# Value and gate projections of the HGRN2 layer moved ahead of its heads, with seven block products for eight

## The chip, the cores and the metric

The kernel runs on one core of a Trainium2 chip. A core has five engines that run side by side, each through its own instructions in program order: TensorE (PE; its weight loads are shown apart as PEld), VectorE (DVE), ScalarE (ACT), GpSimdE (POOL) and SyncE (SP). They wait for each other through semaphores. SP and POOL also issue the DMA transfers here. The metric is the device time of one execution in microseconds. Three runs of the kernel before gave 3575.16, 3577.86 and 3580.52 us; the median is 3577.86 us.

## The reference

A backbone of two layers over 1024 latent tokens and 256 context tokens, model width 1024. Layer 0 has neighbourhood attention and mLSTM heads and isn't touched. Layer 1, cut to what matters (`h` is the normalized, modulated input; T = 1024 latent, 256 context tokens):

```python
q, f_fwd, f_bwd, i, z = split(h @ w_in_c, (2048,) * 5)       # 16 heads of 128 columns each
f = lb + (1 - lb) * sigmoid(f_pre)                            # per direction; k = 1 - f, decay f
q = silu(q)
# per head and direction: S_t = f_t * S_(t-1) + k_t (x) i_t ;  o_t = q_t . S_t
# the state starts from the context tokens; both directions are summed
o = rms(o_fwd + o_bwd, h_norm_c)                              # per head
y = (o * silu(z)) @ w_out_c ;  x = x + gate * y
```

`i` is the value path (V below), `z` the gate path. Only latent tokens leave layer 1, so of the context tokens F and V are needed, not Q and Z.

## The kernel before, in words

Float32 products are made of three passes: every operand is split into a high part and a low remainder of a rounded type, and high x high, high x low and low x high are summed in PSUM. `split` (line 61) makes the two parts: a cast on ACT, a subtraction on DVE. `wblock` and `wring` load and split weights; `wring` uses a ring of four slabs (`wl`, `wh`) of 128x512. `dense` (lines 120 to 122) issues the three matmuls of each of the eight 128-row steps.

`hh` and `hl` hold the transposed `h` of layer 1, all 1280 tokens, in SBUF. In `build`, layer 1 is a loop over 16 heads:

- `hg_proj(h)`: F of both directions and Q, transposed (128 columns of the head by tokens). Eight tiles in PSUM tag `mm`, which has two banks. F goes to `gF` (two halves of 512 tokens) and, for the context, to `gFc`, which has one buffer. ACT takes the sigmoid, DVE scales it. The weights of head 0's F are loaded early, in the last part of layer 0, where its first products are placed too.
- `hg_intra(h)`: inside blocks of 128 tokens, the triangular product A of Q and K by seven levels of doubling blocks (`hg_level`), for two halves of 512 tokens (upper half first). At each level ACT copies a selection of K to `gksel`, TensorE makes four products from it and Q (line 900), DVE writes the masked result into A (line 910, `copy_predicated`) and multiplies K and Q by decays (line 918). Level 0 writes A by a plain multiplication (line 906) and is followed by the diagonal (`hg_diag`). At the end K is transposed (line 879).
- `hg_vz(h)`: V of the context, and for eight tiles of 128 latent tokens V and Z together (256 columns, 24 matmuls a tile); ACT copies V and takes the sigmoid of Z, DVE multiplies (line 821).
- `hg_ctx(h)`: the state of the context, with two scans on DVE that read `gFc` (lines 833, 834).
- `hg_scan(h)`: the states over eight blocks in both directions, the sum in PSUM tag `acc`, the norm (squares on ACT, the root on POOL), times the gate into `gyn` (line 973), four transposes each half (line 976), and a store.

The order on each engine is not that of the code: the scheduler places instructions by priority (earlier code first) and by its own model of time, so products of `hg_vz(h)` stand between the levels of `hg_intra(h)`, and `hg_proj(h+1)` between the steps of `hg_scan(h)`. The order is fixed when the program is built.

Of the kernel before, what the change touches and what calls it, by code (L numbers as in the profile page):

```python
# [9 lines left out]
F32 = mybir.dt.float32  # L10
F32R = mybir.dt.float32r
# [32 lines left out]
class Prog:  # L44
# [727 lines left out]
    def hg_proj(self, h, pool, w=None):  # L772
# [7 lines left out]
        if w:  # L780

            todo.sort(key=lambda x: x[1] == 0)
        w = w or [None, None]
# [17 lines left out]

    def hg_vz(self, h, st, pool):
        nc, a = self.nc, self.a
        col = lambda i: a["wc"][:, i * 2048 + h * P : i * 2048 + (h + 1) * P]
        w = self.wblock(pool, "wz", [col(3), col(4)], KD, 256)
        v = self.t(pool, [P, NT, P], F32, "gv", 2)
        z = self.t(pool, [P, NT - 2, P], F32, "gz", 1)
        ps = self.ps("mm", [P, CTX])
        self.proj_tr(ps, w, 0, LAT, CTX)
        vT = self.t(pool, [P, CTX], F32, "gEc", 1)  # L810
        nc.scalar.copy(vT, ps)
        pt = self.ps("tr", [P, 2, P])
        for j in range(2):
            nc.tensor.transpose(pt[:, j, :], vT[:, j * P : (j + 1) * P], self.ident)
        nc.scalar.copy(v[:, 8:10, :], pt)
        for tt in range(8):
            ps = self.ps("mm", [P, 256])
            self.proj_nat(ps, w, tt, 0, 256)
            nc.scalar.copy(v[:, tt, :], ps[:, 0:P])
            nc.scalar.activation(z[:, tt, :], ps[:, P:256], AF.Sigmoid)  # L820
            nc.vector.tensor_tensor(out=z[:, tt, :], in0=z[:, tt, :], in1=ps[:, P:256], op=ALU.mult)
        st["v"], st["z"] = v, z
# [63 lines left out]
    def hg_level(self, H, lev, pool):  # L886
# [9 lines left out]
        qp = pick(Q)  # L896
        pa = self.ps("s", [P, 4, P])
# [34 lines left out]
    def hg_scan(self, h, st, halves, S, pool, y):  # L932
# [13 lines left out]
        for c in range(8):  # L946
# [22 lines left out]
            self.rsqrt(ss, ss, 1.0 / P)  # L969
            pt = self.ps("tr", [P, 4, P])  # L970
            for i in range(4):
                yn = self.t(pool, [P, P], F32, "gyn", 2)
                nc.vector.scalar_tensor_tensor(
                    out=yn, in0=o4[:, i, :], scalar=ss[:, i : i + 1], in1=z[:, c - 3 + i, :], op0=ALU.mult, op1=ALU.mult
                )
                nc.tensor.transpose(pt[:, i, :], yn, self.ident)
# [5 lines left out]
    def build(self):  # L982
        tc, nc, a = self.tc, self.nc, self.a
        dma = nc.sync.dma_start
        with ExitStack() as es:
# [9 lines left out]
            self.x1 = self.scratch(dr, "x1", [T, D])  # L995
            self.md_all = self.scratch(dr, "md", [20, T, 256])
# [111 lines left out]
            lk = self.fp = l1.enter_context(tc.tile_pool(name="hgk", bufs=1))  # L1108
            with tc.tile_pool(name="op0", bufs=2) as op, ExitStack() as wl:
# [37 lines left out]
                wf = [self.wring([a["wc"][:, 2048 : 2048 + P]], P), None]  # L1147
# [9 lines left out]
                wf[1] = self.wring([a["wc"][:, 4096 : 4096 + P]], P)  # L1157

            with l1:
                pool = l1.enter_context(tc.tile_pool(name="hg", bufs=2))  # L1160
                self.rawp = pool
                l1.enter_context(self.pp.phase(s=3, acc=1))
                st = self.hg_proj(0, pool, wf)
# [33 lines left out]
class _W:  # L1197
# [5 lines left out]
    def part(self, t, k):  # L1203
        return t[k // self.step][:, k % self.step * self.n : (k % self.step + 1) * self.n]
# [123 lines left out]
```

## Time and profile before

| what | value |
|---|---|
| median of three runs | 3577.86 us (3575.16 to 3580.52) |
| profiled execution: span | 3582.2 us |
| PE busy | 3517.0 us, 98% |
| DVE busy | 2216.3 us, 62% |
| ACT busy | 1419.4 us, 40% |
| POOL busy | 456.2 us, 13% |
| mean granted TensorE clock | 0.992 |
| HBM read, written | 241.49 MB, 59.30 MB |

The span is that of one profiled execution, from its first to its last instruction; its own time is that span, 4.3 us above the median of the runs. A row of a timeline gives start, length, engine, source line, operation, output and input by the program's names, and shape. Two rows of one engine can overlap, since the length holds the way through the pipeline; the distance of their starts is what one costs the engine when it has no gap. A row of stretches gives each engine's busy time with the number of instructions, then the granted clock of TensorE and the DMA share. The heads of layer 1 run from about 1955 to 3425 us; layer 1's output product follows.

### The profile page before, as it was taken

What the parts mean: (1) busy time and instruction counts of PE and PEld (TensorE: products, weight loads), DVE (VectorE), ACT (ScalarE), POOL (GpSimd) and SP (SyncE); (2) the same over time, 40 slices, a digit from 0 to 9 for tenths busy, and PEclk for the clock granted to TensorE, in tenths of its full rate; (3) what the DMA queues carried; (4) which work ended last, traced back from release to release, by engine and by line L of the source; (5) the groups of instructions that cost most, each with busy time, mean ns of one, the idle gap of its engine ahead of it and who ended that gap; (6) DMA issues with size and microseconds to landing.
All of it is one profiled execution on the core that took longest, in us unless ns stands there. A gap on an engine that the chain in (4) does not pass through costs nothing.

```text
span 3582.2 us, 65593 instructions
## 1 busy us (share of the span) xinstructions
PE 3517.0 (98%) x24954; PEld 3223.1 (90%) x24954; DVE 2216.3 (62%) x5976; ACT 1419.4 (40%) x3493; POOL 456.2 (13%) x752
## 2 busy tenths in 40 slices
PE   8999999999999999998899999999999999999998
PEld 5879999999999999997788999999999999999877
DVE  5646676666744765655556666666666666666753
ACT  5545555445533333433354333333333333333431
POOL 2222222222211212201010000000000000000000
PEclk9999999999999999999999999999999999999999
DMA  5532222232234434324742111111111111111263
GB/s 211 173 99 77 83 71 81 72 90 76 80 96 145 127 94 140 116 73 149 221 145 77 36 36 34 36 36 36 36 33 36 30 36 36 33 33 36 77 192 117
DMA packets 323051, 305.25 MB, mean 85 GB/s; under 512 B 29016, under 2 KB 280088, under 8 KB 322608
## 3 DMA queue, kind: packets, MB, share of 16 engines
q1 hardware_dynamic: 290704, 217.44, 20.7%
q0 software_dynamic: 32032, 83.61, 6.9%
q8 instruction: 197, 3.23, 0.4%
q14 instruction: 118, 0.97, 0.1%
HBM read 241.49 MB, written 59.30 MB: 84 GB/s over the span
## 4 chain that ended last, share of the span: by engine, by line
PE 85%; issue 6%; DMA 4%; DVE 2%; POOL 1%; ACT 1%; SPq 0%; POOLq 0%; DVEq 0%; ACTq 0%
PE mm L122 18%; PE mm L120 18%; PE mm L121 18%; PE s L900 6%; PE acc L677 2%; PE tr L657 2%; PE mm L731 2%; PE mm L732 2%; PE mm L733 2%; PE acc L461 2%; PE s L470 2%; DMA mld<-md 1%; PE acc L451 1%; PE s L929 1%; PE acc L953 1%
## 5 line engine op out<-in xcount | busy, mean ns | idle before, releaser
L122 PE MATMUL mm<-wh,hl 128*128 128x256 f32 x2560 | 749.6, 293 | 0.3 <-DVE hl L253 0.3
L120 PE MATMUL mm<-wh,hh 128*128 128x256 f32 x2560 | 747.0, 292 | 0.0
L121 PE MATMUL mm<-wl,hh 128*128 128x256 f32 x2560 | 745.9, 291 | 0.0
L122 PEld LDWEIGHTS mm<-wh,hl 128*128 128x128 f32 x2560 | 489.1, 191 | 11.1 <-issue 4.1
L120 PEld LDWEIGHTS mm<-wh,hh 128*128 128x128 f32 x2560 | 489.3, 191 | 7.7 <-issue 1.5
L121 PEld LDWEIGHTS mm<-wl,hh 128*128 128x128 f32 x2560 | 489.2, 191 | 7.1 <-issue 0.5
L120 PE MATMUL mm<-hh,wh 128*128 128x512 f32 (+1 forms) x1216 | 448.3, 369 | 0.0
L121 PE MATMUL mm<-hl,wh 128*128 128x512 f32 (+1 forms) x1216 | 448.3, 369 | 0.0
L122 PE MATMUL mm<-hh,wl 128*128 128x512 f32 (+1 forms) x1216 | 448.1, 368 | 0.0
L122 PE MATMUL mm<-wzh,hl 128*128 128x256 f32 x1024 | 295.3, 288 | 0.0
L120 PE MATMUL mm<-wzh,hh 128*128 128x256 f32 x1024 | 294.2, 287 | 0.0
L121 PE MATMUL mm<-wzl,hh 128*128 128x256 f32 x1024 | 293.9, 287 | 0.0
L895 ACT COPY gksel<-gK 128x512 f32<-128x512 f32 x224 | 149.3, 667 | 315.5 <-PE s L900 159.7
L122 PEld LDWEIGHTS mm<-hh,wl 128*128 128x128 f32 x1216 | 229.7, 189 | 31.4
L120 PEld LDWEIGHTS mm<-hh,wh 128*128 128x128 f32 x1216 | 229.7, 189 | 31.1
L121 PEld LDWEIGHTS mm<-hl,wh 128*128 128x128 f32 x1216 | 229.7, 189 | 30.7
L900 PE MATMUL s<-gQ,gksel 128*128 128x128 f32 x1792 | 254.9, 284 | 0.0
L900 PEld LDWEIGHTS s<-gQ,gksel 128*128 128x128 f32 x1792 | 231.4, 191 | 1.3
L71 ACT CAST wh<-wraw 128x512 fp32r<-128x512 f32 x242 | 148.6, 620 | 202.3 <-PE mm L121 122.5
L731 PE MATMUL mm<-woh,yh 128*128 128x512 f32 x524 | 209.4, 400 | 11.9 <-issue 9.7
L72 DVE TENSOR_TENSOR wl<-wraw,wh 128x512 fp32r<-128x512 f32 x242 | 165.3, 689 | 87.3 <-ACT wh L71 84.9
L733 PE MATMUL mm<-woh,yl 128*128 128x512 f32 x524 | 209.4, 400 | 0.0
(316 smaller groups left out, 7463.0 us busy)
## 6 DMA issues: line engine op xcount, KB each, us to landing
wraw<-yd SPq DMA_DIRECT2D x144, 256.0 KB
wraw<-in_wab_dram SPq DMA_DIRECT2D x112, 256.0 KB
md<-ev POOLq DMA_DIRECT2D x100, 256.0 KB, 2.7
wraw<-in_wc_dram SPq DMA_DIRECT2D x96, 256.0 KB
adar<-in_wada_dram POOLq DMA_DIRECT2D x32, 512.0 KB, 4.6
wraw<-in_wc_dram SPq DMA_DIRECT2D x128, 128.0 KB
adar<-in_wada_dram SPq DMA_DIRECT2D x16, 512.0 KB
wraw<-in_wab_dram SPq DMA_DIRECT2D x64, 128.0 KB
```

The lines of the kernel that those rows point to most:

```text
L71: nc.scalar.copy(hi, x)
L72: nc.vector.tensor_tensor(out=lo, in0=x, in1=hi.bitcast(F32), op=ALU.subtract)
L120: mm(ps, lhsT=lh(k), rhs=rh(k), start=(k == 0), stop=False)
L121: mm(ps, lhsT=lh(k), rhs=rl(k), start=False, stop=False)
L122: mm(ps, lhsT=ll(k), rhs=rh(k), start=False, stop=(k == nk - 1))
L461: nc.tensor.matmul(num, lhsT=qc[:, j, :], rhs=C[d][:, j, :], start=False, stop=(j == 1))
L470: nc.tensor.matmul(u, lhsT=st["k"][c][:, j * P : (j + 1) * P], rhs=vw, start=True, stop=True)
L657: nc.tensor.transpose(pt[:nk, i, :], pr[:, o : o + nk], self.ident)
L731: mm(ps, lhsT=yh[:, k, :], rhs=w.h(kk), start=(kk == 0), stop=False)
L733: mm(ps, lhsT=yl[:, k, :], rhs=w.h(kk), start=False, stop=(kk == 8 * len(qs) - 1))
L895: nc.scalar.copy(ksel.rearrange("p (b s i) -> p b s i", s=2, i=h), pick(K))
L900: nc.tensor.matmul(pa[:, c, :].rearrange("p (b s i) -> p b s i", s=2, i=h), lhsT=ksel[:, c * P : (c + 1) * P], rhs=qp[:, c * nbc : (c + 1) ...
```

## The change

V and Z of all heads are computed before the first head and written to a DRAM scratch `vzd`; a head reads its 128 columns of each back (`hg_vz`). Only V of the context is still computed in the head.

The product is done in eight blocks of 256 columns of V and the same 256 of Z. In block 0 (`q_plain`) it is done as before. In the others (`q_seven`) it is seen as a product of 2x2 blocks: tokens 0 to 511 and 512 to 1023 by the two halves of the inner dimension, and those halves by V and Z. Seven block products (each four token tiles, 12 matmuls of 256 columns a tile) and sums replace eight. The sums on the token side (`q_sums`: four matrices, in high and low parts) are made once, those on the weight side (`q_form`) in each block. Results go through `q_out` (sum, for Z also sigmoid and product) to `vzd`.

In the heads: the gated output overwrites the gate (`gz`, now two buffers) and is transposed by a new function `hg_y`, after the projections of the next head. At level 6 (`lev == 6`, blocks of 64 tokens) ACT copies the selection of Q to a buffer of its own, as it does with K, and the matmuls read the copy. `gF` and `gFc` lie in the heads' pool; head 0's early F weights are replaced by the V weights of block 0.

```diff
-        F = [self.t(p, [P, 2, 512], F32, "gF", 1) for p in (pool, self.fp)]
-        Fc = self.t(self.fp, [P, 2, CTX], F32, "gFc", 1)
+        F = [self.t(pool, [P, 2, 512], F32, "gF", 2) for _ in range(2)]
+        Fc = self.t(pool, [P, 2, CTX], F32, "gFc", 1)
...
+    def q_sums(self, pool):
...
+        for i in range(4):
+            q = lambda x, k, c: x[:, k : k + 4, (i + c) * P : (i + c + 1) * P]
+            o = slice(i * P, (i + 1) * P)
+            def part(n, r):
+                nc.scalar.copy(S[n][0][:, :, o], r)
+                tt(S[n][1][:, :, o], r, S[n][0][:, :, o].bitcast(F32), ALU.subtract)
...
+    def q_form(self, raw, n, add=None):
+        w = _W([], [], 2, 256)
+        for i in range(2):
+            if add:
+                self.nc.vector.tensor_tensor(out=raw[n][i], in0=raw[n][i], in1=raw[add][i], op=ALU.add)
+            w.lo.append(self.t(self.wp, [P, 512], F32R, "wl", self.slabs))
+            w.hi.append(self.t(self.wp, [P, 512], F32R, "wh", self.slabs))
+            self.split(w.hi[i], w.lo[i], raw[n][i])
+        return w
+
+    def q_mul(self, ps, a, w, first, last):
+        mm = self.nc.tensor.matmul
+        ah, al = a
+        for k in range(4):
+            mm(ps, lhsT=ah[:, k, :], rhs=w.h(k), start=first and k == 0, stop=False)
+            mm(ps, lhsT=ah[:, k, :], rhs=w.l(k), start=False, stop=False)
+            mm(ps, lhsT=al[:, k, :], rhs=w.h(k), start=False, stop=last and k == 3)
...
+    def q_seven(self, j, S, pool):
...
+        for i, ps in product(lambda i: self.q_h(i, 0), self.q_form(raw, "11")):
+            u[i] = self.t(pool, [P, 256], F32, "qu", 4)
+            nc.scalar.copy(u[i], ps)
+        for i, ps in product(lambda i: self.q_h(i, 1), self.q_form(raw, "21")):
+            self.q_out(pool, i, j, 0, u[i], ps, ALU.add)
+        for i, ps in product(s("1"), self.q_form(raw, "11", "12")):
+            m5[i] = ps
+        for i, ps in product(s("2"), self.q_form(raw, "11", "22")):
+            tt(out=u[i], in0=u[i], in1=ps, op=ALU.add)
+            v[i] = self.t(pool, [P, 256], F32, "qv", 4)
+            tt(out=v[i], in0=m5[i], in1=u[i], op=ALU.subtract)
+        for i, ps in product(s("3"), self.q_form(raw, "12", "22")):
+            self.q_out(pool, i + 4, j, 1, v[i], ps, ALU.subtract)
+            tt(out=u[i], in0=u[i], in1=ps, op=ALU.add)
+        for i, ps in product(lambda i: self.q_h(i + 4, 1), self.q_form(raw, "11", "21")):
+            self.q_out(pool, i + 4, j, 0, u[i], ps, ALU.add)
+        for i, ps in product(s("4"), self.q_form(raw, "22")):
+            self.q_out(pool, i, j, 1, v[i], ps, ALU.add)
...
     def hg_vz(self, h, st, pool):
-        w = self.wblock(pool, "wz", [col(3), col(4)], KD, 256)
...
+        for t, i in ((v, 0), (z, 1)):
+            nc.sync.dma_start(
+                out=t[:, 0:8, :], in_=self.vzd[i, :, h * P : (h + 1) * P].rearrange("(c p) f -> p c f", p=P)
+            )
...
-        for tt in range(8):
-            ps = self.ps("mm", [P, 256])
-            self.proj_nat(ps, w, tt, 0, 256)
-            nc.scalar.copy(v[:, tt, :], ps[:, 0:P])
-            nc.scalar.activation(z[:, tt, :], ps[:, P:256], AF.Sigmoid)
-            nc.vector.tensor_tensor(out=z[:, tt, :], in0=z[:, tt, :], in1=ps[:, P:256], op=ALU.mult)
...
+        if lev == 6:
+            qsel = self.t(pool, [P, n], F32, "gksel", 3).rearrange("p (b s i) -> p b s i", s=2, i=h)
+            nc.scalar.copy(qsel, qp)
+            qp = qsel
...
+    def hg_y(self, h, st, pool, y):
+        nc = self.nc
+        for c in (0, 4):
             pt = self.ps("tr", [P, 4, P])
             for i in range(4):
+                nc.tensor.transpose(pt[:, i, :], st["z"][:, c + i, :], self.ident)
...
             with l1:
+                self.nq = 0
+                with tc.tile_pool(name="qv", bufs=1) as pool, self.pp.phase(sa=4):
+                    self.q_plain(0, early, pool)
+                    S = self.q_sums(pool)
+                    for j in range(1, 8):
+                        self.q_seven(j, S, pool)
...
                 for h in range(16):
                     hv = self.hg_intra(st, pool)
                     self.hg_vz(h, st, pool)
                     S = self.hg_ctx(st, pool)
-                    self.hg_scan(h, st, hv, S, pool, self.yd2)
+                    self.hg_scan(h, st, hv, S, pool)
+                    done = st
                     if h < 15:
                         st = self.hg_proj(h + 1, pool)
+                    self.hg_y(h, done, pool, self.yd2)
```

More of the change, by code (lines that the diff above doesn't have):

```diff
@@ L1146, in build @@
                 self.slabs = 4
-                wf = [self.wring([a["wc"][:, 2048 : 2048 + P]], P), None]
+                early = []
+                for k in range(2):
+                    rows = a["wc"][k * 512 : (k + 1) * 512, 3 * 2048 : 3 * 2048 + 256]
+                    early.append(self.wblock(self.wp, "w", [rows], 4, 256, op, ring=self.slabs))
                 for tt in [8, 9, 4, 5, 6, 7, 0, 1, 2, 3]:
```

104 lines of the change are left out of this document (89 added, 15 removed).

## The prediction

> **What bounds the kernel now.** I read the page first, then stretches of layer 1, then one head in order of time.
>
> ```profile
> span 3582.2 us, 65593 instructions
> PE 3517.0 (98%) x24954; PEld 3223.1 (90%) x24954; DVE 2216.3 (62%) x5976; ACT 1419.4 (40%) x3493; POOL 456.2 (13%) x752
> PE   8999999999999999998899999999999999999998
> ```
> TensorE is busy nearly everywhere. The busy time of stretches (columns: stretch, its length, then each engine) says the same of the layer boundary (second row), of five heads (first) and of the inside of one head (last):
>
> ```profile
> 2500.00:2961.00 461.00, 461.00 (x3252) 430.37 (x3251) 301.80 (x750) 149.94 (x366) 21.38 (x30) 1.00 0.12 35
> 1900.00:1950.00 50.00, 50.00 (x259) 42.94 (x258) 30.28 (x76) 23.98 (x55) 2.20 (x5) 1.00 0.26 78
> 2139.60:2176.20 36.60, 36.60 (x319) 36.60 (x318) 30.55 (x80) 14.27 (x35) 0.60 (x1) 1.00 0.02 9
> L833 DVE TENSOR_TENSOR_SCAN gEc<-gFc,gzero x16: 683/684/684, 1990.8 to 3371.9; 128x255 f32<-128x255 f32 x16
> ```
> L833 runs once a head, so a head takes (3371.9 - 1990.8) / 15 = 92.1 us, all of it TensorE's. The stretch 2139.60 to 2176.20 is one head's `hg_intra` from the lower half's level 0 to the two context scans of `hg_ctx`. There DVE works 30.55 of 36.6 us: TensorE leads only because V and Z products fill the places where it would wait for DVE. The same stretch for the tile `wzl`, one of the three matmuls of each product step:
>
> ```profile
> 2139.60:2176.20 36.60, 16.70 (x58) 10.93 (x58) 0.00 (x0) 1.00 0.02 9
> 2079.85 0.28 PE L120 MATMUL mm<-wzh,hh 128*128 128x256 f32 x1
> 2081.98 0.28 PE L120 MATMUL mm<-wzh,hh 128*128 128x256 f32 x1
> ```
> So 3 x 58 = 174 fill matmuls stand in it. Between the two timeline rows lie 18 steps in 2.13 us: a 256-wide matmul holds TensorE for 0.118 us. The fill is 174 x 0.118 = 20.5 us of the 36.6.
>
> **The change, part by part.**
>
> *Products.* Before, V and Z take 16 heads x 8 tiles x 24 = 3072 matmuls. After, the plain block has 2 x 8 x 24 = 384 and the seven others 7 products x 4 tiles x 12 = 336 each, 2736 in all. TensorE saves 336 x 0.118 = **39.6 us**. The context rows of V (24 matmuls a head) stay.
>
> *The heads lose their fill.* This decides. TensorE runs its instructions in program order, and that order in the changed kernel is the same in every middle head (`hg_intra` and what follows, in matmuls of the program; level and diagonal ones run as two passes):
>
> ```
> level 0 lower x4, diagonal x8 with 4 late transposes, level 1 upper x4
> context half of the next head's F (256 wide) x18, level 1 lower x4, the same x6
> levels 2 to 5, both halves: x32, nothing between
> K transposes x8, level 6 upper x4, K transposes x8, level 6 lower x4
> V transposes x2, first scan product x1, then the next head's F (512 wide) x20 ...
> ```
> Only 24 narrow matmuls are left between the levels. More can't come: two PSUM banks serve tag `mm`. The next head's two context products hold them, because their result goes to `gFc`, which has one buffer, and this head's scans read that at the end of the stretch. So DVE now sets the time. One level of one half, in order:
>
> ```profile
> 2145.23 0.73 DVE L910 COPY_PREDICATED gA<-glm,s 128x512 f32<-128x512 uint8 x1
> 2145.84 0.76 DVE L918 TENSOR_TENSOR gQ<-gQ,gT 128x256 f32<-128x256 f32 x2
> 2146.51 0.76 DVE L918 TENSOR_TENSOR gK<-gK,gT 128x256 f32<-128x256 f32 x2
> 2147.18 0.74 DVE L910 COPY_PREDICATED gA<-glm,s 128x512 f32<-128x512 uint8 x1
> 2063.94 1.05 PE L900 MATMUL s<-gQ,gksel 128*128 128x128 f32 x8
> 2064.75 0.36 PE L122 MATMUL mm<-wzh,hl 128*128 128x256 f32 x1
> ```
> DVE needs 2147.18 - 2145.23 = 1.95 us for what TensorE does in 0.81 us (from its first matmul to the next work). For the whole stretch I take the measured busy time and change it:
>
> ```profile
> 2140.93 0.60 DVE L973 SCALAR_TENSOR_TENSOR gyn<-acc,gss,gz 128x128 f32<-128x128 f32 x2
> 2141.45 0.75 DVE L918 TENSOR_TENSOR gK<-gK,gT 128x256 f32<-128x256 f32 x2
> 2145.03 0.28 DVE L821 TENSOR_TENSOR gz<-gz,mm 128x128 f32<-128x128 f32 x1
> L790 DVE TENSOR_SCALAR gF<-gF,lb 128x512 f32<-128x512 f32 x57 | 30.9, 542 | 1.4 <-ACT gF L789 1.4
> L789 ACT ACTIVATE gF<-mm 128x512 f32<-128x512 f32 x58 | 34.5, 595 | 106.1 <-PE mm L122 105.5
> L895 ACT COPY gksel<-gK 128x512 f32<-128x512 f32 x196 | 130.6, 667 | 282.9 <-PE s L900 140.7 <-issue 67.4 <-DVE gK L861 41.1
> L789 ACT ACTIVATE gFc<-mm 128x256 f32<-128x256 f32 x28 | 10.8, 385 | 70.4 <-PE mm L122 70.4
> ```
> DVE: 30.55, less 8 gate products (0.20 each until the next starts, 1.6), less two `gyn` (0.52), plus one F correction that now falls here (about 0.5): 28.9 us. Waits in its queue come on top. In ACT's order the evacuation of F (0.60) stands ahead of the level 1 copy of K (0.67), and both follow DVE's last use of the old F: the next K product waits 1.3 us. At level 6 the lower half's Q copy stands behind two evacuations of K transposes: about 1.0. Then ACT evacuates the context product (0.39) before a bank is free. Together 31.6 us.
>
> TensorE in the same stretch: 36.6 - 20.5 + 24 x 0.118 (2.8) = 18.9 us. It idles 31.6 - 18.9 = 12.7, say **13 us a head**, 16 x 13 = **208 us**. Bounds: below, levels 2 to 6 alone, 10 x 1.95 = 19.5 us of DVE against 10 x 0.81, 16 transposes of about 0.11 and six narrow matmuls (10.6 in all), so 9 us; above, those three waits twice (2.7 more) and one more pair on ACT ahead of the bank (1.3), so 17. I take 13, from the stretch itself. In the rest of a head, 55.5 us, 18 fill matmuls (2.1 us) go too; DVE has 92.1 x 301.80 / 461 - 30.55 = 30 us of work there, and scans, projections and transposes keep their order, so it stays TensorE's. A head then takes 92.1 - 192 x 0.118 + 13 = 82.5 us.
>
> *The new stage.* Each seven-product block gives DVE 14 splits and 8 sums of weights, 128x512, and 36 operations of 128x256.
>
> ```profile
> 2114.48 0.68 DVE L908 TENSOR_TENSOR gksel<-gK 128x512 f32<-128x512 f32 x1
> 2115.09 0.42 DVE L920 TENSOR_TENSOR gT<-gT 128x256 f32<-128x256 f32 x1
> 2115.43 0.76 DVE L918 TENSOR_TENSOR gK<-gK,gF 128x256 f32<-128x256 f32 x2
> ```
> At 0.61 and 0.34 that is 13.4 + 12.2 = 25.6 us under 336 x 0.118 = 39.6 us of TensorE: hidden. ACT has 14 casts (0.62 by its row at L71, which the next fence shows) and 12 evacuations, less than DVE. `q_sums` adds 56 x 0.61 = 34 us of DVE and 16 copies on ACT, once, after the last tile of h. From there DVE has 34 us, 5 us of the plain block (4 splits, 8 gate products) and 25.6 us, 65 in all, until block 1 is done; TensorE has 96 + 192 + 336 matmuls, 73.6 us. With a wait of up to 0.6 us for each of the 16 copies the two come out level, and I take 6 us of stall; bounds 0 and, were the cover gone, 34. Where the stage hands its memory to the heads, the first weights of head 0 go from load to cast to split with nothing else for TensorE: 6 us; bounds 0 and 12 (two such chains in a row).
>
> ```profile
> L71 ACT CAST wh<-wraw 128x512 fp32r<-128x512 f32 x86 | 53.1, 620 | 105.6 <-PE mm L121 105.6
> L72 DVE TENSOR_TENSOR wzl<-wraw,wzh 128x512 fp32r<-128x512 f32 x58 | 40.1, 691 | 115.4 <-ACT wzh L71 115.4
> ```
> *Edits that cost nothing.* The 128 stores on POOL's queue and 32 reloads on SP's replace weight loads of equal size (1 MB a head; DMA share 0.12 in the heads). In SP's queue the reload of z waits for the late transposes of two heads before, and the next F weights queue behind it; these transposes are done early in the preceding `hg_intra`, tens of us ahead. The two Q copies (0.67) are ACT's, which works 150 of 461 us; one is in the tail above. The late transposes are the same eight; before, no TensorE time was idle for them to lose. At the layer boundary plain V products replace head 0's projection as fill: TensorE was full there and stays so.
>
> **Sum.** 3582.2 - 39.6 + 208 + 12 = 3762.6 in terms of the profiled execution, which stands 4.3 us over the median of the runs (3577.86). So **3758 us**.
>
> **Rivals.**
>
> *The half clock joins in (0.12).* Granted clock in neighbouring stretches (the eighth column of figures, ahead of DMA share):
>
> ```profile
> 3374.50:3377.90 3.40, 1.52 (x13) 1.37 (x12) 2.40 (x5) 2.60 (x5) 0.00 (x0) 1.00 0.80 228
> 3378.00:3381.30 3.30, 3.30 (x9) 2.31 (x8) 2.37 (x6) 1.77 (x3) 0.00 (x0) 0.50 0.88 206
> 220.60:224.00 3.40, 1.61 (x14) 1.40 (x12) 1.28 (x2) 1.15 (x2) 2.41 (x4) 1.00 0.51 129
> 224.00:227.40 3.40, 0.00 (x0) 0.00 (x0) 0.00 (x0) 0.00 (x0) 2.96 (x5) 1.00 0.31 88
> ```
> A stretch of 3.40 us in which TensorE was busy 1.52 us is followed by one at 0.50; after one with 1.61 us (third row) the next is still at 1.00. The levels would be busy 1.05 of 1.95 us, just above that; the end of the stretch, with some 2 us of waiting, can fall under it. A spell of 3.4 us at half clock costs 1.7 us of full work: 16 x 1.7 = 27, so 3785. The Trainium skill, "TensorE: Matmul & The Clock Gate", section "What's actually happening", has the clock halved after at least one idle window of about 3.4 us; by that rule no spell would come, as no wait is so long. The trace differs: its stretch was 45% busy.
>
> *The new stage is DVE's (0.12).* If the 34 us of sums are not covered, 3758 + 28 = 3786. For it: DVE and TensorE are level there. Against: 9 us of room before waits.
>
> *The fill suffices (0.05): faster.* If DVE's work in the levels overlapped with other TensorE work as now, only 39.6 - 12 are left: 3550. It decides when idle per head falls under 27.6 / 16 = 1.7 us. For it: a head still has eight projection tiles and the context's V to spread. Against: their place in the order above.
>
> *The change doesn't do what it says (0.02).* Its saving and its stalls cancel, 3578: idle at 1.7 us.
>
> **How the numbers follow.** My forecast has 0.66, and 0.03 goes to slower cases that I don't name. Range 3682 (9 us idle, no stalls in the new stage: 3582.2 - 39.6 + 144 - 4.3) to 3835 (17 us: 3822, and 13 of the uncovered sums); its top takes in both slower rivals. A measurement can tell 0.2%, 7 us, from no change. Faster 0.05, same 0.02, slower 0.93.
>
> **What the profile after would show.** A stage of some 330 us with TensorE full; then heads 82 to 83 us apart by the context scan, TensorE near 84% busy, with idle ahead of the level matmuls ended by DVE's `gQ` and a last wait of 1 to 3 us ahead of the 512-wide F products; TensorE's share near 93%. I'm wrong if the heads are under 78 us apart, or if TensorE's idle lies elsewhere.

## The result, and the profile after

The changed kernel takes 3805.35 us (median of four runs, 3800.36 to 3808.09), the kernel before 3579.19 us beside it (four runs). The ratio is 1.063, with a 95% interval of 1.0615 to 1.0645: slower by 226 us. The page of the profiled execution:

```profile
span 3806.3 us, 65773 instructions
PE 3575.2 (94%) x24618; PEld 3221.9 (85%) x24618; DVE 2383.2 (63%) x6294; ACT 1477.0 (39%) x3459; POOL 514.8 (14%) x880
PE   8999999999999999988879999899999899998989
```

TensorE has 336 matmuls fewer and still ends 226 us later. Slices are 95 us long. Of the dip 8 8 8 7 in the middle the last two (1808 to 1998 us) are the end of the layer boundary, which had nines before; its first two stand in both kernels. Four nines of the new stage follow, and then the heads, with an 8 now and then where the kernel before had nines throughout.

**The heads.** The context scan, once a head, and the busy time of five heads (columns as in the rows of stretches before):

```profile
L960 DVE TENSOR_TENSOR_SCAN gEc<-gFc,gzero x16: 682/684/686, 2393.8 to 3639.2; 128x255 f32<-128x255 f32 x16
2850.00:3265.00 415.00, 378.09 (x2339) 336.15 (x2339) 284.56 (x713) 137.17 (x292) 19.58 (x32) 0.98 0.16 47
```

A head takes (3639.2 - 2393.8) / 15 = 83.0 us. Fourteen of the fifteen periods are 80.5 to 82.4 us and the last is 107.4, because part of layer 1's output product now runs in it. "Busy" (378.09 of 415.00 us) is 91%, which is too high, because the modelled end of the last matmul before a wait covers part of that wait. The distance from each matmul's start to the next one's start hides nothing. I summed it in both traces over the twelve heads between the third and the fifteenth context scan, by what the matmul makes, and divided by twelve (us a head):

```
                                        before    after   change
V and Z of latent tokens                  24.1        -    -24.1
F, Q, V of the context                    43.1     43.2     +0.1
products of the levels                    12.5     21.6     +9.1
transposes of K                            1.6      2.7     +1.1
contexts (k, states, V's transposes)       1.4      1.9     +0.5
states and sums of the scan                7.2      9.2     +2.0
diagonal, transposes of the output         2.3      2.6     +0.3
head                                      92.2     81.2    -11.0
```

So 24.1 us of work left a head, and 13.1 us of it came back as waiting, 9.1 us of that at the levels. Their timeline in one head (start, length, engine, line; in brackets the idle time before and what ended it) and TensorE's waits in the five heads (us, times, longest):

```profile
2863.33 1.13 PE L1031 MATMUL s<-gQ,gksel 128*128 128x128 f32 x8 [0.82 <-ACT gksel L1022]
2865.28 1.13 PE L1031 MATMUL s<-gQ,gksel 128*128 128x128 f32 x8 [0.82 <-ACT gksel L1022]
2867.23 1.13 PE L1031 MATMUL s<-gQ,gksel 128*128 128x128 f32 x8 [0.82 <-ACT gksel L1022]
```

```profile
PE s L1031 <- ACT gksel L1022: 21.4, 26, 0.8
PE mm L120 <- ACT gFc L786: 5.6, 5, 1.1
PE s L1031 <- DVE gQ L1049: 3.6, 5, 0.8
```

The levels come 1.95 us apart, which is the length of VectorE's set for one level and half. The copy of K on ScalarE that ends the wait stands behind VectorE's product of K. In the scan 2.0 us more a head are lost.

**The layer boundary.** Two stretches of the last output products of layer 0, in the kernel after (the kernel before has TensorE busy for all 50.00 us of both), and then the loads of their left operands (`wraw<-yd`: lowest, median and longest issue in ns, first and last start) with the idle time that ended at these loads (us, times), first after, then before:

```profile
1800.00:1850.00 50.00, 39.61 (x152) 26.64 (x153) 20.84 (x45) 17.97 (x42) 2.83 (x7) 0.97 0.28 84
1850.00:1900.00 50.00, 42.12 (x189) 31.02 (x188) 20.92 (x52) 19.32 (x50) 2.69 (x6) 0.97 0.32 99
```

```profile
L718 SPq DMA_DIRECT2D wraw<-yd x40: 359/360/377, 1787.5 to 1968.4; - x40
  DMA wraw<-yd: 81.1, 37
```

```profile
L718 SPq DMA_DIRECT2D wraw<-yd x40: 359/365/917, 1781.8 to 1891.5; - x40
  DMA wraw<-yd: 4.0, 4
```

Forty loads come 4.6 us apart in place of 2.8, and the casts wait for 37 of them. The buffers `wraw` are three. The change loads four raw tiles of V weights ahead of these products, and their split parts need four slabs of the ring, of which two hold output weights (`rings[14:] = [(self.wp, "w", 4)] * 2`) until the last output tile. So two of the raw tiles can't be split, and they hold two of the three buffers all the while. The loads run through the one that is left, and the way of each load through memory is exposed.

**The new stage and the hand-over.** The stage's main stretch, and TensorE's waits from 1700 to 2400 us:

```profile
2000.00:2300.00 300.00, 299.28 (x2512) 298.87 (x2511) 216.90 (x450) 102.60 (x203) 62.44 (x116) 1.00 0.28 97
```

```profile
PE mm L731 <- ACT yh L71: 36.5, 36, 3.1
PE mm L731 <- issue: 13.2, 1, 13.2
PE mm L120 <- ACT wh L71: 7.6, 1, 7.6
PE sa L863 <- ACT qo L878: 4.6, 1, 4.6
PE sa L863 <- ACT s2h L812: 0.6, 1, 0.6
```

The stage is TensorE's. It waits 0.6 us for the operand sums; the 4.6 us wait for the copy `qo` stands ahead of that, in the plain block at 1988 us. Where the stage gives way to the heads it waits 7.6 us for the first weights.

### The profile page after: what moved, and what is told of

It reads as the page before. It is cut to its first block, busy times and chain, and to the rows that moved or that the text cites. A ratio compares the mean times of both kernels' runs of the same rounds, so it can differ in the third digit from the quotient of the medians.

```text
span 3806.3 us, 65773 instructions
## 1 busy us (share of the span) xinstructions
PE 3575.2 (94%) x24618; PEld 3221.9 (85%) x24618; DVE 2383.2 (63%) x6294; ACT 1477.0 (39%) x3459; POOL 514.8 (14%) x880
## 4 chain that ended last, share of the span: by engine, by line
PE 62%; issue 14%; DVE 11%; DMA 7%; POOL 3%; ACT 2%; SPq 0%; POOLq 0%; ACTq 0%; DVEq 0%
PE mm L120 13%; PE mm L122 13%; PE mm L121 13%; DMA wraw<-yd 3%; DVE gQ L1049 3%; DVE gA L1041 3%; DVE gK L1049 2%; PE s L1031 2%; PE acc L677 2%; PE tr L657 2%; POOL vzd L883 2%; PE s L470 1%; PE acc L461 1%; PE mm L731 1%; PE mm L733 1%
## 5 line engine op out<-in xcount | busy, mean ns | idle before, releaser
L120 PE MATMUL mm<-hh,wh 128*128 128x512 f32 (+1 forms) x1344 | 487.6, 363 | 24.6 <-ACT gFc L786 16.8
L121 PE MATMUL mm<-hl,wh 128*128 128x512 f32 (+1 forms) x1344 | 485.3, 361 | 0.0
L122 PE MATMUL mm<-hh,wl 128*128 128x512 f32 (+1 forms) x1344 | 485.0, 361 | 0.0
L120 PEld LDWEIGHTS mm<-hh,wh 128*128 128x128 f32 x1344 | 255.7, 190 | 61.6 <-ACT gFc L786 19.7
L72 DVE TENSOR_TENSOR wl<-wraw,wh 128x512 fp32r<-128x512 f32 x278 | 189.9, 689 | 152.1 <-ACT wh L71 149.7
L122 PEld LDWEIGHTS mm<-hh,wl 128*128 128x128 f32 x1344 | 255.7, 190 | 34.6
L121 PEld LDWEIGHTS mm<-hl,wh 128*128 128x128 f32 x1344 | 255.8, 190 | 33.7
L731 PE MATMUL mm<-woh,yh 128*128 128x512 f32 x524 | 216.2, 413 | 55.6 <-ACT yh L71 38.2
L1022 ACT COPY gksel<-gK 128x512 f32<-128x512 f32 x224 | 148.7, 664 | 234.5 <-DVE gA L1041 94.3
L733 PE MATMUL mm<-woh,yl 128*128 128x512 f32 x524 | 215.5, 412 | 0.4 <-DVE yl L72 0.4
L732 PE MATMUL mm<-wol,yh 128*128 128x512 f32 x524 | 211.3, 404 | 0.0
L731 PEld LDWEIGHTS mm<-woh,yh 128*128 128x128 f32 x524 | 101.1, 193 | 90.7 <-ACT yh L71 55.9
L71 ACT CAST yh<-wraw 128x512 fp32r<-128x512 f32 x144 | 86.7, 619 | 217.4 <-DMA wraw<-yd 123.8
```

Of the source, the lines that this page charges most:

```text
L71: nc.scalar.copy(hi, x)
L72: nc.vector.tensor_tensor(out=lo, in0=x, in1=hi.bitcast(F32), op=ALU.subtract)
L120: mm(ps, lhsT=lh(k), rhs=rh(k), start=(k == 0), stop=False)
L121: mm(ps, lhsT=lh(k), rhs=rl(k), start=False, stop=False)
L122: mm(ps, lhsT=ll(k), rhs=rh(k), start=False, stop=(k == nk - 1))
L731: mm(ps, lhsT=yh[:, k, :], rhs=w.h(kk), start=(kk == 0), stop=False)
```

## The experiments

Four questions: does the boundary's loss come from the raw buffers, is the loss in the heads VectorE's, why does no other work fill it, and what are the change's other parts worth.

**1. Second half of the early V weights late.**

```diff
-                for k in range(2):
-                    rows = a["wc"][k * 512 : (k + 1) * 512, 3 * 2048 : 3 * 2048 + 256]
-                    early.append(self.wblock(self.wp, "w", [rows], 4, 256, op, ring=self.slabs))
+                rows = lambda k: a["wc"][k * 512 : (k + 1) * 512, 3 * 2048 : 3 * 2048 + 256]
+                early.append(self.wblock(self.wp, "w", [rows(0)], 4, 256, op, ring=self.slabs))
                 for tt in [8, 9, 4, 5, 6, 7, 0, 1, 2, 3]:
...
+                early.append(self.wblock(self.wp, "w", [rows(1)], 4, 256, op, ring=self.slabs))
```

> The changed kernel with one edit: of block 0's early V weights only the first half is loaded ahead of the last output tiles of layer 0, the second half after them. Theory (raw buffers): the second half needs two slabs of ring `w` that the output weights hold to the end, so its two raw tiles keep two of the three `wraw` buffers and the loads of `yd` go through one. Then the loads of `yd` come every 2.7 us again instead of every 4.2 us, the waits of TensorE's L731 for ACT (36 us) go, and the time falls by 50 to 62 us, to 3745 to 3755. Rival (the V products themselves, or the bytes of their weights, disturb that stage): they are all still there, so the time falls by less than 10 us.

Measured: 3741.03 us (3738.55 to 3747.48), ratio 1.0455 (1.0439 to 1.0470), 64 us less than after and 4 us below the theory's range. The same rows of its trace:

```profile
L718 SPq DMA_DIRECT2D wraw<-yd x40: 359/365/717, 1780.0 to 1889.2; - x40
  DMA wraw<-yd: 3.6, 2
```

The loads come 2.8 us apart again. A head stays at 81.1 us by the sums of starts.

**2. The same tiles early, in raw buffers of their own.**

```diff
+                    how = dict(rawb=2, rawt="eraw") if k else {}
-                    early.append(self.wblock(self.wp, "w", [rows], 4, 256, op, ring=self.slabs))
+                    early.append(self.wblock(self.wp, "w", [rows], 4, 256, op, ring=self.slabs, **how))
```

> The changed kernel with one edit: the raw tiles of the second half of block 0's early V weights have a tag of their own with two buffers; when they are loaded and where they are split is left. Theory (raw buffers): as with the second half loaded late, the time falls by 50 to 62 us, to 3745 to 3755. Rival (not the buffers but the slab ring: the splits of that half stand in ACT's and DVE's queues and block what is behind them): the time falls by less than 15 us.

Measured: 3741.93 us (3736.70 to 3742.31), ratio 1.0451 (1.0435 to 1.0467). With the early loads in their place and only the buffers parted, the gain is the same 63 us. So the raw buffers are the cause, and the place of these weights in the ring and in the queue costs nothing that can be seen.

**3. `gFc` in two buffers.** The prediction gave one reason why no projections stand between the levels: the next head's context products hold both `mm` banks until `gFc` is free.

```diff
-        Fc = self.t(pool, [P, 2, CTX], F32, "gFc", 1)
+        Fc = self.t(pool, [P, 2, CTX], F32, "gFc", 2)
```

> The changed kernel with one edit: `gFc` has two buffers. Theory (the missing fill): the next head's context products no longer hold both `mm` banks, so its projections stand between the levels; DVE still needs 31 us for its stretch, but TensorE works through it. A head falls from 81.3 us to 71 to 75, the time by 90 to 150 us, to 3655 to 3715. Rival (DVE and the chain of copies set a head whatever stands between the levels, the scan taking its own time without fill): a head stays over 79 us, the time falls by less than 35 us.

Measured: 3798.64 us (3794.86 to 3805.65), ratio 1.0609 (1.0592 to 1.0627), only 7 us less than after: the number is the rival's (less than 35 us, a head over 79 us), the theory's 90 to 150 us was missed. Its heads, and TensorE's waits in the same stretch:

```profile
2850.00:3265.00 415.00, 381.23 (x2371) 340.39 (x2370) 287.33 (x722) 137.30 (x304) 21.30 (x35) 0.97 0.16 47
PE tr L967 <- DVE gq L963: 14.7, 5, 3.3
PE s L1031 <- DVE gQ L991: 7.2, 6, 1.2
PE acc L1083 <- DVE gA L1041: 5.3, 5, 1.6
```

The order did change as the prediction's reason has it: 512-wide products stand between the levels, and the waits for `gksel` L1022 are gone from the list. But others took their place: for the contexts' k (L967), for the next head's Q (L991), for the last level's A (L1083). The sums of starts by kind, for this run and those that follow (us a head, as above). The last row is the time in a head at half clock, by the granted clock of the traces; it is contained in the rows above it and comes in spells of 3.41 us:

```
                                 before  after  no Q-decay  gFc two  Q ahead  own k  GpSimd  contexts first
F, Q, V of the context             43.1   43.2        44.2     45.0     45.4   44.0    43.6            43.2
products of the levels             12.5   21.6        14.4     14.1     14.2   13.8    14.1            13.1
transposes of K                     1.6    2.7         2.0      2.4      1.8    2.0     1.7             1.7
contexts                            1.4    1.9         3.4      3.1      3.6    1.7     1.9             3.9
states and sums of the scan         7.2    9.2         8.0     13.1     11.4   12.7    11.8            15.8
transposes of the output            0.6    0.8         0.8      1.2      0.6    0.4     0.4             3.5
diagonal                            1.7    1.8         1.7      1.7      1.7    1.7     1.7             1.8
head                               92.2   81.2        74.5     80.4     78.5   76.5    75.6            83.0
of it at half clock                 0.0    3.4         2.8      5.4      6.8    1.5     0.6            10.2
```

With `gFc` in two buffers the levels lose 7.5 us of waiting; the scan takes 3.9 us more, the projections 1.8, the contexts 1.2. The products that now fill the levels stood beside the scan and the contexts before, and are missing there. The time at half clock grew by 2.0 us a head, so a part of what the scan takes more is the clock's; the run doesn't part the two.

**4. Both together.**

```diff
-        Fc = self.t(pool, [P, 2, CTX], F32, "gFc", 1)
+        Fc = self.t(pool, [P, 2, CTX], F32, "gFc", 2)
...
+                early.append(self.wblock(self.wp, "w", [rows(1)], 4, 256, op, ring=self.slabs))
```

> Both edits, the late second half and two `gFc` buffers. If the two causes are apart, the gains add: 3590 to 3665. If the missing fill is all that heads lost, 3590 to 3620; if the first edit only shifts a wait into the new stage, 3650 to 3715.

Measured: 3730.22 us (3726.42 to 3732.61), ratio 1.0421 (1.0405 to 1.0436). That is 75 us less than after: the 64 of experiment 1 and 11 more for `gFc`. So the two causes are apart, but none of the expected ranges was met, since the second gain is as small here as in experiment 3.

**5. Less of VectorE in the levels**, on top of experiment 1. The kernel leaves out the products of Q and the decay.

```diff
             (Kv, 0, 0, Tv[:, 0, :, 1]), (Kv, 1, 1, Tv[:, 1, :, 0]),
-            (Qv, 0, 0, Tv[:, 1, :, 1]), (Qv, 1, 1, Tv[:, 0, :, 0]),
```

> The kernel after with the second half of the early V weights loaded late, and without the two products a level and half that multiply Q by the decay (28 of VectorE's instructions a head; the output is then not the reference's). TensorE's work is the same. Theory (VectorE's sets between the levels pace the head, 1.95 us a level and half, of which these two are 0.66): a head loses 14 x 0.66 = 9.2 us less what TensorE then needs itself, so it comes from 81.3 to 72-75 us and the kernel from 3741 to 3595-3640 us. Rival (something else ends last in the heads: the chain across heads, the contexts' sigmoid, the scan): under 3 us a head, the kernel at 3693-3741 us.

Measured: 3636.60 us (3631.96 to 3641.46), ratio 1.0154 (1.0138 to 1.0169), 104 us under the kernel of experiment 1 or 6.5 us a head, within the theory's range. Its heads, and TensorE's longest waits there:

```profile
2850.00:3265.00 415.00, 404.08 (x2549) 361.81 (x2548) 258.64 (x623) 147.90 (x317) 21.30 (x35) 0.98 0.17 51
PE mm L120 <- ACT gFc L786: 9.0, 5, 1.8
PE s L1031 <- ACT gksel L1022: 1.2, 8, 0.2
```

With 28 instructions of VectorE fewer a head and all of TensorE's, in nearly the same order (56 of the levels' matmuls follow each other with nothing between, 64 in after), the levels take 14.4 us in place of 21.6 and the wait for `gksel` falls from 21.4 to 1.2 us in five heads. VectorE's sets between the levels are what TensorE waits for in the changed kernel.

**6. All blocks plain**, on top of experiment 1.

```diff
-                    S = self.q_sums(pool)
                     for j in range(1, 8):
-                        self.q_seven(j, S, pool)
+                        self.q_plain(j, None, pool)
```

> The kernel after with the second half of the early V weights loaded late, and all eight column blocks by eight plain products, with no operand sums and none of the seven-product combinations. It parts the saving by seven products from the move of V and the gates out of the heads. Theory (the new stage is TensorE's): 336 more 256-wide matmuls at 0.118 us, less about 1 us of stalls for the sums, so 3741 + 39 = 3780 us (3773-3785). Rival (the stage's evictions, sums or stores set its pace and take part of the saving): less than 25 us more, under 3766 us.

Measured: 3779.81 us (3778.32 to 3780.70), ratio 1.0552 (1.0535 to 1.0570), 38.8 us more than experiment 1, as the theory has it. Seven products for eight save what their matmuls take. Without them, moving V and Z out of the heads costs 3779.81 - 3580.85 (the kernel before beside it) = 199 us.

**7. The small edits alone**, in the kernel before.

```diff
+        if lev == 6:
+            qsel = self.t(pool, [P, n], F32, "gksel", 3).rearrange("p (b s i) -> p b s i", s=2, i=h)
+            nc.scalar.copy(qsel, qp)
+            qp = qsel
...
-                    self.hg_scan(h, st, hv, S, pool, self.yd2)
+                    self.hg_scan(h, st, hv, S, pool)
+                    done = st
                     if h < 15:
                         st = self.hg_proj(h + 1, pool)
+                    self.hg_y(h, done, pool, self.yd2)
```

> The kernel before, with V and the gates still in the heads, and with the small edits alone: a head's output written in its gates' place, the transposes after the next head's projections, Q copied plain at the 64-blocks. The prediction costed all these at nothing. Theory: 3572-3586 us, a head at 92 us, TensorE full. Rival: the late transposes or the copy cost a wait in a full head: above 3590 us; or they take away a wait of the scan: below 3565 us.

Measured: 3579.59 us (ten runs, 3576.36 to 3582.02), ratio 0.9995 (0.9986 to 1.0005). They cost nothing in a kernel whose TensorE is full; a head by the context scan is (3367.2 - 1987.0) / 15 = 92.0 us:

```profile
L833 DVE TENSOR_TENSOR_SCAN gEc<-gFc,gzero x16: 683/684/686, 1987.0 to 3367.2; 128x255 f32<-128x255 f32 x16
```

**8. Q and A of the next head ahead**, on top of experiment 4: is it the buffers that the scan still reads that keep the levels late?

```diff
-            Q = self.t(pool, [P, 2, n], F32, "gQ", 2)
+            Q = self.t(pool, [P, 2, n], F32, "gQ", 4)
-            A = self.t(pool, [P, 4, P], F32, "gA", 2)
+            A = self.t(pool, [P, 4, P], F32, "gA", 3)
```

> The kernel after with the second half of the early V weights loaded late, gFc in two buffers, and besides gQ in four buffers and gA in three, so that the next head's Q and its first levels need not wait until the scan has read this head's. Theory (the heads are held by a chain across them: Q and A of a head are free only when its scan has read them, so the levels start late, have used up their fill before they end, and TensorE idles at their end): a head comes from 80 us to 73-77 us, towards the 69.4 us of TensorE's work in it (92.1 less 22.7), and the kernel from 3730 to 3620-3685 us. Rival (the levels end late because VectorE is full while they run, the fill's own evictions included, whatever buffers there are): a head stays at 79-81 us and the kernel at 3720-3740 us.

Measured: 3696.58 us (3693.89 to 3697.16), ratio 1.0319 (1.0304 to 1.0335), 34 us less, below the rival's range and above the theory's. The chain across heads is there and is worth 1.8 us a head (80.3 to 78.5). The wait for k at the levels' end stays (L967 <- `gq` L963: 13.5 us in five heads).

**9. The contexts' k in a buffer of its own**, on top of experiment 8.

```diff
-        k = self.t(pool, [P, 2, CTX], F32, "gq", 2)
+        k = self.t(pool, [P, 2, CTX], F32, "gkc", 1)
-            A = self.t(pool, [P, 4, P], F32, "gA", 3)
+            A = self.t(pool, [P, 4, P], F32, "gA", 2)
```

> The kernel of e3_q_ahead, with the contexts' k in a buffer of its own and not in one of the two of gq (gA back to two buffers). In e3_q_ahead the next head's second q must wait for this head's contexts, which come behind the last level, so one whole projection (24 matmuls, 5.5 us) can't be done while the levels run. Theory (TensorE idles at the end of the levels for want of work that may run there): the last levels and the contexts get 512-wide products beside them, a head comes from 79.2 to 73-77 us, the kernel from 3697 to 3600-3665 us. Rival (VectorE is full there and everything waits for it, whatever TensorE could do meanwhile comes back as idle time later): 3680-3705 us.

Measured: 3673.84 us (3673.54 to 3674.00), ratio 1.0264 (1.0247 to 1.0281), 23 us less; a head takes 76.5 us, within the theory's 73 to 77, the kernel 9 us above its range. TensorE's waits in five heads of it:

```profile
2850.00:3265.00 415.00, 396.12 (x2489) 351.22 (x2488) 307.70 (x772) 145.95 (x308) 20.32 (x31) 0.99 0.17 50
PE mm L120 <- ACT gFc L786: 11.9, 5, 2.4
PE s L1031 <- DVE gA L1037: 3.9, 5, 0.8
```

The wait for k is gone from the contexts (3.6 to 1.7 us), part of it came back in the scan (11.4 to 12.7). The time at half clock falls from 6.8 to 1.5 us a head. By the 1.6 us that one spell of 3.41 us costs in this kernel (last section), that is an estimated 2.5 us, no less than the 1.9 us that the head gains: the shorter wait seems to count mostly through the clock, which no run parts from it.

**10. The contexts ahead of the levels**, on top of experiment 9.

```diff
-                    hv = self.hg_intra(st, pool)
                     self.hg_vz(h, st, pool)
                     S = self.hg_ctx(st, pool)
+                    hv = self.hg_intra(st, pool)
```

> The kernel of e7_own_k, with V's context product and the contexts' states ahead of the levels and not behind them. TensorE's wait for k at the end of the levels (13.5 us in five heads of e3_q_ahead, 2.7 us a head, with the half-clock spell that follows it) must vanish. Theory (that wait is the head's last loss): 73-76 us a head, 3590-3650 us. Rival (the fill that stood beside the contexts is used up in the levels, and the scan at the head's end is left without: the wait turns up there, at its states): 77-80 us a head, 3660-3710 us.

Measured: 3770.23 us (3764.15 to 3776.75), ratio 1.0534 (1.0517 to 1.0550), 96 us more than experiment 9, far beyond what either theory gave. The rival named the mechanism and undersized it. The waits of five heads, and two neighbouring stretches where one head goes over to the next:

```profile
PE tr L1112 <- DVE gz L1103: 32.9, 10, 3.5
PE tr L967 <- DVE gkc L963: 8.2, 5, 1.7
```

```profile
2890.00:2894.00 4.00, 1.80 (x7) 1.43 (x8) 1.34 (x3) 1.27 (x2) 0.61 (x1) 0.50 0.62 199
2894.00:2898.00 4.00, 4.00 (x21) 4.00 (x21) 1.47 (x4) 0.00 (x0) 0.00 (x0) 0.50 0.00 0
```

Of the 216 projection matmuls of the head from 2806 us on, 144 stand in the levels and 72 beside the first states of the scan. The rest of the scan (15.8 us in all for 7.2 of work) and the transposes behind it (3.5 for 0.6) run bare, the clock falls to half there, and the next head's first levels run at half.

**11. Some of VectorE's work given to ScalarE**, on top of experiment 9.

```diff
-            nc.vector.tensor_scalar(out=dst, in0=dst, scalar1=olb, scalar2=lb, op0=ALU.mult, op1=ALU.add)
+            nc.scalar.activation(dst, dst, AF.Identity, scale=olb, bias=lb)
...
-            nc.vector.tensor_scalar(out=K, in0=F, scalar1=-1.0, scalar2=1.0, op0=ALU.mult, op1=ALU.add)
+            nc.scalar.activation(K, F, AF.Copy, scale=-1.0, bias=1.0)
```

> The kernel of e7_own_k with two jobs of VectorE in the heads given to ScalarE: the lower bound put on the gates' F (15.7 us in five heads of e7_own_k, 3.1 us a head) and K = 1 - F (7.0 us in five heads, 1.4 us a head). TensorE's work is the same. In e4_no_q_decay 9.2 us less of VectorE took 6.5 us off a head. Theory (VectorE's work in the levels still sets the head): 4.5 x 0.7 = 3.2 us a head, the kernel from 3674 to 3615-3635 us. Rival (ScalarE's copies of K between the levels come later for the 5 us it takes on, and the levels wait for them): 3660 us or more.

Measured: 3670.73 us (3667.14 to 3671.46), ratio 1.0252 (1.0236 to 1.0267). No gain that counts (3 us for 51 expected). The number is the rival's, but its reason isn't shown: the levels take 14.1 us for 13.8.

**12. The weight splits given to GpSimd besides.**

```diff
-        nc.vector.tensor_tensor(out=lo, in0=x, in1=hi.bitcast(F32), op=ALU.subtract)
+        e = nc.gpsimd if getattr(self, "heads", False) else nc.vector
+        e.tensor_tensor(out=lo, in0=x, in1=hi.bitcast(F32), op=ALU.subtract)
```

> The kernel of e9_scalar_takes_some with the low parts of the heads' weight splits besides given from VectorE to GpSimd (27.6 us of VectorE in five heads of e7_own_k, 5.5 us a head). Theory (any microsecond that VectorE is spared in the heads is worth about 0.7): 3.9 us a head more, 3555-3575 us, under the kernel before. Rival (GpSimd's long operations beside VectorE's slow these down, or the splits come too late for the products that need them): not below e9_scalar_takes_some by more than 20 us, or above it.

Measured: 3660.43 us (3657.49 to 3661.53), ratio 1.0226 (1.0209 to 1.0243), 10 us less than experiment 11 for 62 expected, as the rival has it. Groups of VectorE's K products in experiment 9 (first) and here (second), and GpSimd's splits (third; busy us, mean ns):

```profile
L1049 DVE TENSOR_TENSOR gK<-gK,gT 128x256 f32<-128x256 f32 x136 | 51.4, 421 | 1.1 <-ACT gksel L1022 1.1
```

```profile
L1050 DVE TENSOR_TENSOR gK<-gK,gT 128x256 f32<-128x256 f32 x132 | 59.5, 492 | 0.6
L73 POOL TENSOR_TENSOR wl<-wraw,wh 128x512 fp32r<-128x512 f32 x46 | 63.3, 1376 | 216.2 <-ACT wh L71 201.9 <-ACT gkn L1009 13.8
```

From experiments 11 and 12 the rate of 0.7 us a head for each microsecond of VectorE, taken from experiment 5, doesn't carry over. In experiment 5 most of the levels had no work beside them; from experiment 9 on they are filled (13.8 us for 12.5 of work) and most of the loss sits in the scan. That this is why the rate fell is argued, not shown. None of these versions beats the kernel before. Whether an order exists that fills both the levels and the scan from the 43 us of projections stays open: moving the contexts alone made it worse (experiment 10), and an order written by hand wasn't tried.

## Why the prediction was right or wrong, by its steps

The time of 3805 us lies in the range and on the side that was forecast, 47 us above the value of 3758. That distance is the difference of a term that is missing (64 us) and of terms that were too large (together some 20 us). That these partly made up for it was luck.

- **Edits that cost nothing: the layer boundary. This step failed.** "Plain V products replace head 0's projection as fill: TensorE was full there and stays so" looked at what TensorE would have to do and not at what the early weights hold. They cost 64 us (experiments 1 and 2). The lines to see it stand in the code: three raw buffers, four slabs, two of them taken until the last output tile.
- **Edits that cost nothing: the rest.** The late transposes, the gate's overwriting and the Q copy cost nothing in the kernel before (experiment 7, ratio 0.9995). In five heads of the changed kernel TensorE waits 3.1 us for the Q copy at L1026, 0.6 a head; the prediction had it inside its 13 us, at about 1.0. The stores and reloads weren't run alone; none of TensorE's waits in these heads ends at one.
- **The heads lose their fill: 13 us a head.** Measured 13.1 (81.2 - 92.2 + 24.1). The place is right in the main, 9.1 us of it at the levels at 1.95 us each, and so is the cause there: VectorE's sets (experiment 5). But 2.0 us lie in the scan, where the prediction expected no loss, so the levels and what follows them up to the scan lost some 11 us, where the prediction gave them 12.7. V and Z took 24.1 us a head and not the 192 x 0.118 = 22.7 of the sum. So a head came to 81.2 us and not 82.5; taken against 22.7 the loss is 11.7 us, and the agreement of 13.1 with 13 is in part luck. By the sums of starts TensorE works 68.1 of 81.2 us, the 84% of the forecast; the row of busy time shows 91%. The wait before the levels is ended by the copy `gksel` behind VectorE's product of K, more often than by `gQ`. The wait ahead of the 512-wide products is 1.1 us at most, of 1 to 3 forecast.
- **"More can't come": wrong as a reason.** The two banks held for `gFc` were what kept the products out of the levels, but letting them in gained 7 us of the 208 (experiment 3; 11 in experiment 4), since the same products were missing afterwards beside the scan and the contexts. More buffers on top took a head from 80.3 to 76.5 us with the same work (experiments 8 and 9). Whether the 8.4 us that are left over 68.1 of work are want of work or a matter of order stays open.
- **16 heads.** The last one loses about as much as the others, but elsewhere. Its levels have the output product beside them (198 matmuls at L731 to L733 in the stretch 3531.8 to 3639.2, 192 of them in three lines like the one below; none between the last two context scans of the kernel before). Its scan then has nothing beside it: from 3640.7 to 3665.4 us TensorE does about 9 us of work (by the kernel before's sums) in 24.7. The sums of starts over the whole kernel, before against experiment 6, give 206 us of waiting in all sixteen heads, close to the 208 of the forecast. V and Z themselves take 379 us as a stage, its two waits of 2.9 and 7.4 us included, for 385 in the heads: 0.120 us a matmul for 0.125. Together that is 200 us, and experiment 6 measures 199 for moving them. The cheaper matmuls, some 16 us that the sum didn't have, are most of what it gave too much.

```profile
L731 PE MATMUL mm<-woh,yh 128*128 128x512 f32 x64 | 26.7, 419 | 2.2 <-ACT woh L71 2.0 <-ACT yh L71 0.3
```

- **Products: 39.6 us saved.** Measured 38.8 (experiment 6 against 1). **The new stage:** 6 us of stall for the sums were about 1. The hand-over's 6 us were 7.6.
- **The half clock joins in** (a rival at 0.12, 27 us): in part true. Between the first and the last context scan the trace of after has sixteen spells of 3.41 us at half clock, the trace of before none (one behind its last scan). The four heads with a spell right behind their context scan take 82.1 to 82.4 us; the ten others up to the last take 80.5 to 81.9, eight with a spell in their levels and two without. So a spell costs some 1.6 us behind the scan and less in the levels, where TensorE waits for VectorE anyway. It is contained in the 13.1. The stage isn't VectorE's, and the fill doesn't suffice: these two rivals fell.

## What to carry to other kernels

Before moving work out of a loop, list every chain that it stood beside (here levels, contexts and scan) and say what will stand there instead, counting the fill that is left only once: where filling one chain empties the next, the wait moves more than it shrinks. A load put ahead of a running loop holds its staging buffer until its own destination is free; compare the buffers it pins with those the loop needs.

## What the runs showed of the hardware

The half clock comes at about half load, with no long wait at all. Four neighbouring stretches of one head of the kernel after (granted clock in the eighth column of figures):

```profile
2862.50:2865.90 3.40, 1.76 (x14) 1.62 (x14) 3.40 (x11) 1.24 (x2) 0.00 (x0) 1.00 0.00 0
2865.90:2869.30 3.40, 1.75 (x14) 1.43 (x13) 3.40 (x10) 1.24 (x2) 0.00 (x0) 1.00 0.00 0
2869.30:2872.70 3.40, 3.37 (x15) 3.11 (x16) 3.40 (x10) 0.62 (x1) 0.00 (x0) 0.50 0.00 0
2872.70:2876.10 3.40, 2.52 (x20) 2.20 (x19) 3.40 (x10) 0.62 (x1) 0.00 (x0) 0.99 0.00 0
```

TensorE idles 0.82 us at a time there and is busy 1.75 us of 3.40 (by records whose ends are modelled, so rather less in truth), and the next 3.41 us are granted at half. The stretch before it, with 1.76 us, wasn't followed by one. Of the sixteen spells, the fourteen ahead of the last head follow 3.41 us with 1.71 to 1.78 us of busy time (the two in the last head 1.99 and 1.46); up to there some stretches of 3.41 us with 1.77 or 1.78 us, and all with 1.79 us or more, are followed by full speed. The Trainium skill, "TensorE: Matmul & The Clock Gate", section "What's actually happening", has the slow state after at least one idle window of about 3.4 us. The length of the window agrees; that it must be idle doesn't, since it was half busy here. Levels paced at 1.95 us lie just at the border.

What a spell costs shows best in the kernel of experiment 9. Two neighbouring heads of it, from context scan to context scan, with the same matmuls in the same order, the second with one spell of 3.41 us behind its scan:

```profile
2810.51:2886.36 75.85, 72.07 (x458) 64.01 (x458) 55.57 (x143) 26.51 (x57) 3.94 (x6) 1.00 0.17 50
2886.36:2963.84 77.48, 73.70 (x458) 65.14 (x458) 55.60 (x142) 26.51 (x57) 3.94 (x6) 0.98 0.16 48
```

That is 1.6 us for a spell. From the second to the thirteenth period of this trace, the six without a spell take 75.8 or 75.9 us and the six with one behind the scan 77.3 to 77.5.

GpSimd's subtraction of 128x512 takes 1.38 us where VectorE's takes 0.69. The Trainium skill, "Trainium Architecture — The Big Picture", section "The five engines, in one table", calls it two times slower for such work; the trace agrees. The mean of VectorE's K products in experiment 12, 0.49 us in place of 0.42, hides two cases: of the 132, 123 took 0.42 us and nine 1.51. Each of the nine started 0.06 to 0.35 us after a subtraction of GpSimd's and ended 0.28 us after it. One of them (the second of the two K products in the first row):

```profile
3021.36 1.85 DVE L1050 TENSOR_TENSOR gK<-gK,gT 128x256 f32<-128x256 f32 x2
3021.63 1.30 POOL L73 TENSOR_TENSOR wl<-wraw,wh 128x512 fp32r<-128x512 f32 x1 [1.70 <-ACT wh L71]
```

So single products were held up until GpSimd was done, by over 1 us each, and the others were not slowed.
